# Moving the transfers of turned h, in the second gate/up product, from SyncE's queue to GpSimd's

## The chip, the core and the metric

One core of a Trainium2 chip runs the whole layer as one program. The metric is device time in microseconds (us), from start to end of the program. The kernel before takes 1830.62 us, the median of three runs (1828.49 to 1831.59).

The engines have short names here: PE (TensorE, matrix products), DVE (VectorE), ACT (ScalarE), POOL (GpSimd) and SP (SyncE, which only issues transfers). Each engine takes its instructions in the order of its own queue. A transfer (DMA) is issued from the queue of an engine and then runs beside it.

## The reference

A layer on x of 256 rows by 2048 columns in float32: half a feed-forward net, a mixer (a state-space group beside stick-breaking attention), half a feed-forward net again, and a gated per-layer embedding. The change lies in the second feed-forward net:

```python
def swiglu(h, w_gate, w_up, w_down):
    return (jax.nn.silu(h @ w_gate) * (h @ w_up)) @ w_down

x = x + 0.5 * swiglu(rms_norm(x, ffn2_norm[i]), ffn2_w_gate[i], ffn2_w_up[i], ffn2_w_down[i])
```

w_gate and w_up are 2048 x 5632, w_down is 5632 x 2048.

## The kernel before

**Halves.** A float32 product is made of three products of a rounded type: every operand is split in a high half (a cast on ACT, line 181) and a low half (what the cast lost, a subtraction on DVE, line 184). For weights the tiles are called whi/wlo or shi/slo, in seven pairs that are used in turn; raw is the weight tile as it came from memory (128 x 2048, 1 MB, five buffers). A raw buffer is free again when the last split that reads it has ended.

**Blocks.** Gate and up columns are worked in eleven blocks f = 0 to 10 of 512 columns each. In the second feed-forward net (`bg` is None there) the blocks from 1 on use the class `Wide`. Its `seven` takes a fast scheme with seven products in place of eight: weights of gate and up are added to each other on DVE (line 697, tile sum), one addition is made by an accumulating transfer from one raw buffer into another (line 704, from POOL's queue), and seven products run on PE (lines 666, 670 and 672). Between some products ACT hands a bank over with its sign turned (line 679). What is left of the 2048 rows is multiplied in the plain way by `column` (lines 325, 328 and 334): in even blocks two quarters of the rows, in odd blocks, where `seven` takes a third tile too ("joined"), one quarter.

**Loads.** Weights come through SP's queue: line 634 for the tiles of `seven`, line 315 for the columns, line 526 for the same in the down product.

**Order of a block.** `seven`, gate columns, up columns. When the gate columns are done, ACT applies silu (line 795, tile sg); when the up columns are done, DVE forms h = silu(gate) * up (lines 799 and 805).

**Steps.** Small pieces of work are put beside the products: `step()` is called after every product of `seven` and after every half of a column, and each generator in the list `beside` advances by one then. Steps set the place in program order only. The compiler orders each engine's queue itself, by its estimate of when things become ready, and may move a ready instruction ahead of one that waits.

**Turning h.** The down product needs h with its columns along the partitions. Two steps into the block after f, `turned` runs: DVE transposes h in squares of 32 (`turn_blocks`, line 217) into the tile mid. After each odd f, and after the last one, `turn_quarters` places the turned rows with 16 transfers of 32 partitions (line 230) into the tile hT of the pair of blocks. These transfers are issued in four groups of four, after 8 steps more. An even block has 7 + 8 = 15 steps, so the groups stand in its last four. mid has one buffer; hT is read by the down product only, as the tile hhi and others. `turn_quarters` is called from `Normed.block` too, for x (tile h, other step counts).

**After the gate/up product.** `fetch_x` (line 150) brings x back through POOL's queue, in eight transfers, into two of the five raw buffers; the down product runs with its own accumulating transfers (line 580) from POOL.

Of the kernel before, what the change touches and what calls it, by code (L numbers as in the profile page):

```python
# [33 lines left out]
def layer_kernel(ctx: ExitStack, tc: tile.TileContext, a: dict, shapes: dict, out: bass.AP):  # L34
    nc = tc.nc
# [31 lines left out]
    def get(pool, tag, width=1024, bufs=1):  # L67
        return pool.tile([P, width], F32, tag=tag, name=uid(tag), bufs=bufs)

    def com(tag):  # L70
        return get(comp, tag, *{"sg": (1024, 1), "h": (1024, 2), "sq": (NB, 1), "mid": (2048, 1)}[tag])
# [23 lines left out]
    def start(g):  # L95
        beside.append(g)
        return g
# [117 lines left out]
    def turn_blocks(mid, src, t, k0, nk):  # L215

        nc.vector.transpose(
            mid[:, :, t, k0 : k0 + nk, :].rearrange("p q f b -> p f q b"),
            src.rearrange("p (f q b) -> p f q b", f=nk, q=4),
        )  # L220

    def turn_quarters(out, mid, steps):


        def g():
            for _ in range(steps):
                yield
            for i in range(4):
                for q in range(4):
                    nc.sync.dma_start(  # L230
                        out[32 * q : 32 * q + 32].rearrange("p (t i w) -> p t i w", t=TT, i=4)[:, :, i],
                        mid[32 * i : 32 * i + 32, q].rearrange("p t f b -> p t (f b)"),
                    )
                yield

        return start(g())

    def by_tile(out, nk):

        return out.rearrange("p (x f b) -> p f x b", f=nk, b=32)  # L240
# [142 lines left out]
    class Normed:  # L383
# [12 lines left out]
        def block(self, n):  # L396
            if self.laid:
                ps = self.laid(n)
            elif n < self.early:

                if n % 2 == 0 or self.mid is None:
                    self.mid = com("mid")
                mid = self.mid[:, n % 2 * 1024 : n % 2 * 1024 + 1024].rearrange(
                    "p (q t f b) -> p q t f b", q=4, t=TT, b=32
                )
                out = com("h")
                for t in range(TT):
                    turn_blocks(mid, xt[t][n], t, 0, 4)
                soon = n >= ND - 2
                turn_quarters(out, mid, 4 if soon else 6)  # L410
                put_off(9 if soon else 11, self.parted, n, by_tile(out, 4))
                put_off(1, self.squares, n)
                return
            else:
                ps = aux()
                for t in range(TT):
                    for j in range(4):
                        pin(nc.tensor.transpose(
                            ps[:, j * T + t * P : j * T + (t + 1) * P], xt[t][n][:, j * P : (j + 1) * P], ident
                        ))  # L420
            self.parted(n, ps.rearrange("p (j s) -> p j s", j=4))
            if not self.laid:
                put_off(1, self.squares, n)
# [317 lines left out]
    def ffn(i, xn, nxt, bg=None):  # L741
# [11 lines left out]
        mids = {}  # L753
# [5 lines left out]
        def turned(hp, f, hh):  # L759
            pair, n_pair = f // 2, min(2, NF - f // 2 * 2) * 4  # L760
            if f % 2 == 0:
                mids[pair] = com("mid")[:, : 128 * TT * n_pair].rearrange(
                    "p (q t f b) -> p q t f b", q=4, t=TT, b=32
                )
            for t in range(TT):
                turn_blocks(mids[pair], hh[:, t * NB : (t + 1) * NB], t, f % 2 * 4, 4)
            if f % 2 or f == NF - 1:
                hf = get(hp, f"hT{pair}", T * n_pair)
                turn_quarters(hf, mids[pair], 8)
                hT.append(by_tile(hf, n_pair))  # L770

        for f in range(NF):
# [9 lines left out]
            if not bg and f:  # L782
# [10 lines left out]
                def gate(s=s, sg=sg):  # L793
# [6 lines left out]
                    out=hh.rearrange("p (t n) -> p t n", t=TT), in0=s.double.rearrange("p (t n) -> p t n", t=TT),  # L800
                    in1=five.unsqueeze(1).to_broadcast([P, TT, NB]), op=ALU.add,
                )
                for t in range(TT):
                    cols = slice(t * NB, (t + 1) * NB)
                    nc.vector.scalar_tensor_tensor(
                        out=hh[:, cols], in0=hh[:, cols], scalar=xn.rs(t), in1=sg[:, cols], op0=ALU.mult, op1=ALU.mult
                    )
                if f == NF - 2:
                    side.close()
                    hp = pools.enter_context(phase(f"h{i}b"))  # L810
                put_off(2, turned, hp, f, hh)
                continue
            if bg and (f >= early or f in alone):
# [28 lines left out]
                def ended(s, g=gate_cols, u=up_cols, hh=hh, f=f, hp=hp):  # L842
                    nc.vector.tensor_tensor(out=hh, in0=s.banks[3.8], in1=hh, op=ALU.add)
                    for t in range(TT):
                        nc.vector.scalar_tensor_tensor(
                            out=u[t], in0=u[t], scalar=xn.rs(t), in1=g[t], op0=ALU.mult, op1=ALU.mult
                        )
                    put_off(2, turned, hp, f, hh)
# [37 lines left out]
            for t in range(TT):  # L886
                nc.vector.scalar_tensor_tensor(
                    out=hh[:, t * NB : (t + 1) * NB], in0=pu[t], scalar=xn.rs(t),
                    in1=sg[:, t * NB : (t + 1) * NB], op0=ALU.mult, op1=ALU.mult,
                )  # L890
            put_off(2, turned, hp, f, hh)

        fetch_x(a["x"][0] if bg else scr_x)
# [805 lines left out]
    for n, side in ((0, 0), (1, 0), (0, 1), (1, 1), (2, 0), (2, 1), (3, 0), (3, 1)):  # L1699
        y, r = ((yss, rss), (ysb, rsb))[side]  # L1700
        ps = next(both) if n < 2 and not side else gemm_block(lambda k: y[k], sides[side], n * NB, SW // P)
        for t in range(TT):
            nc.vector.scalar_tensor_tensor(
                out=xt[t][n], in0=ps[t], scalar=r[0][:, t : t + 1], in1=xt[t][n], op0=ALU.mult, op1=ALU.add
# [127 lines left out]
    for c, (ahead, total) in enumerate(((early, part), (part, ms))):  # L1832
# [3 lines left out]
            out=com("sq")[:, :W], in0=gate[:, cols[c]], scalar=1.0, in1=gate[:, cols[c]], op0=ALU.mult, op1=ALU.mult,  # L1836
# [129 lines left out]
```

## Time and profile before

| | before |
|---|---|
| median of three runs | 1830.62 us |
| the profiled execution's own time | 1830.58 us |
| its span, first to last instruction | 1828.8 us |
| granted TensorE clock | 0.999 |
| PE busy | 1809.7 us (99%) |
| DVE busy | 1561.9 us (85%) |
| ACT busy | 1090.9 us (60%) |
| POOL busy | 110.9 us (6%) |

A row of a group or of a timeline reads: start, duration, engine, line, operation, tile written <- tiles read, shape, count, and in brackets the idle time of the engine before it with what ended that. Times are us from the start of the span. "SPq" is an issue on SP's queue. A row of waits reads: who waited <- for whom: total us, how often, the longest. A matmul row lasts 0.39 us but the next one starts 0.23 us after it: they are pipelined, so the distance of starts is what a matmul costs.

### The profile page before, as it was taken

What the parts mean: (1) busy time and instruction counts of PE and PEld (TensorE: products, weight loads), DVE (VectorE), ACT (ScalarE), POOL (GpSimd) and SP (SyncE); (2) the same over time, 40 slices, a digit from 0 to 9 for tenths busy, and PEclk for the clock granted to TensorE, in tenths of its full rate; (3) what the DMA queues carried; (4) which work ended last, traced back from release to release, by engine and by line L of the source; (5) the groups of instructions that cost most, each with busy time, mean ns of one, the idle gap of its engine ahead of it and who ended that gap; (6) DMA issues with size and microseconds to landing.
All of it is one profiled execution on the core that took longest, in us unless ns stands there. A gap on an engine that the chain in (4) does not pass through costs nothing.

```text
span 1828.8 us, 24199 instructions
## 1 busy us (share of the span) xinstructions
PE 1809.7 (99%) x8894; PEld 1492.1 (82%) x8894; DVE 1561.9 (85%) x1809; ACT 1090.9 (60%) x1282; POOL 110.9 (6%) x166
## 2 busy tenths in 40 slices
PE   9999999999999999999999999999999999999998
PEld 7888888888888888888898888777877788888887
DVE  8978889999998896696567889989898998889875
ACT  7445456555665665455794675666566756566664
POOL 0020100000000001010020000000000010000000
PEclk9999999999999999999999999999999999999999
DMA  8799866787775667574646778677777686666663
GB/s 323 268 293 302 262 213 230 239 273 219 254 281 200 203 235 257 178 260 150 225 142 225 250 240 294 220 262 231 247 234 242 224 281 232 230 201 225 207 236 127
DMA packets 108230, 430.49 MB, mean 235 GB/s; under 512 B 24432, under 2 KB 48400, under 8 KB 65712
## 3 DMA queue, kind: packets, MB, share of 16 engines
q1 hardware_dynamic: 96256, 390.06, 60.3%
q0 software_dynamic: 11136, 37.49, 9.5%
q8 instruction: 69, 1.13, 0.3%
q10 hardware_dynamic: 720, 1.41, 0.2%
q14 instruction: 49, 0.40, 0.1%
HBM read 372.41 MB, written 10.88 MB: 210 GB/s over the span
## 4 chain that ended last, share of the span: by engine, by line
PE 87%; DVE 5%; issue 3%; DMA 2%; ACT 2%; POOL 0%; ACTq 0%; DVEq 0%; POOLq 0%
PE acc L325 15%; PE acc L334 15%; PE acc L328 15%; PE aux L325 6%; PE aux L328 6%; PE aux L334 6%; PE acc L512 2%; PE acc L513 2%; PE acc L515 2%; DVE wlo L184 2%; PE acc L666 2%; PE aux L515 2%; PE acc L670 2%; PE aux L512 2%; PE aux L513 2%
## 5 line engine op out<-in xcount | busy, mean ns | idle before, releaser
L184 DVE TENSOR_TENSOR wlo<-raw,whi 128x1024 fp32r<-128x1024 f32 x483 | 584.0, 1222 | 132.1 <-ACT whi L181 131.7
L181 ACT CAST whi<-raw 128x1024 fp32r<-128x1024 f32 x483 | 502.0, 1050 | 304.0 <-PE acc L328 188.0
L325 PE MATMUL acc<-whi,nhi 128*128 128x512 f32 x880 | 346.5, 394 | 1.1 <-ACT whi L277 0.9
L328 PE MATMUL acc<-whi,nlo 128*128 128x512 f32 x880 | 343.6, 390 | 0.0
L184 DVE TENSOR_TENSOR slo<-raw,shi 128x1024 fp32r<-128x1024 f32 x183 | 222.4, 1215 | 32.1 <-ACT shi L181 31.0
L334 PE MATMUL acc<-wlo,nhi 128*128 128x512 f32 x880 | 243.8, 389 | 0.1
L181 ACT CAST shi<-raw 128x1024 fp32r<-128x1024 f32 x183 | 192.0, 1049 | 64.5 <-DMA raw<-in_ffn_w_down 17.7
L325 PEld LDWEIGHTS acc<-whi,nhi 128*128 128x128 f32 x880 | 165.7, 188 | 37.9 <-ACT whi L277 1.9
L334 PEld LDWEIGHTS acc<-wlo,nhi 128*128 128x128 f32 x880 | 165.3, 188 | 35.0 <-DVE wlo L184 0.5
L328 PEld LDWEIGHTS acc<-whi,nlo 128*128 128x128 f32 x880 | 165.8, 188 | 33.6
L181 ACT CAST whi<-sum 128x1024 fp32r<-128x1024 f32 x88 | 92.3, 1051 | 122.5 <-DVE sum L519 61.9
L184 DVE TENSOR_TENSOR wlo<-sum,whi 128x1024 fp32r<-128x1024 f32 x88 | 106.7, 1219 | 8.0 <-ACT whi L181 7.3
L181 ACT CAST shi<-sum 128x1024 fp32r<-128x1024 f32 x62 | 65.2, 1052 | 69.2 <-DVE sum L519 35.2
L325 PE MATMUL aux<-whi,nhi 128*128 128x512 f32 x216 | 84.0, 389 | 0.0
L328 PE MATMUL aux<-whi,nlo 128*128 128x512 f32 x216 | 84.0, 389 | 0.0
L184 DVE TENSOR_TENSOR slo<-sum,shi 128x1024 fp32r<-128x1024 f32 x62 | 75.6, 1219 | 1.3 <-ACT shi L181 1.0
L325 PE MATMUL aux<-whi,hhi 128*128 128x512 f32 x176 | 68.5, 389 | 0.0
L328 PE MATMUL aux<-whi,hlo 128*128 128x512 f32 x176 | 68.5, 389 | 0.0
L334 PE MATMUL aux<-wlo,nhi 128*128 128x512 f32 x216 | 65.2, 389 | 0.0
L519 DVE TENSOR_TENSOR sum<-sum,raw 128x1024 f32<-128x1024 f32 x50 | 61.0, 1220 | 0.8
L580 POOL DMA_DIRECT2D raw<-raw x23 | 19.9, 866 | 634.3 <-DVE sum L519 364.7
L697 DVE TENSOR_TENSOR sum<-sum,raw 128x1024 f32<-128x1024 f32 x50 | 58.4, 1217 | 0.0
(466 smaller groups left out, 3488.0 us busy)
## 6 DMA issues: line engine op xcount, KB each, us to landing
raw<-in_ffn_w_up SPq DMA_DIRECT2D x88, 1024.0 KB, 6.8
raw<-in_ffn_w_down SPq DMA_DIRECT2D x88, 1024.0 KB, 4.9
raw<-in_ffn_w_gate SPq DMA_DIRECT2D x86, 1024.0 KB, 6.9
raw<-in_w_in SPq DMA_DIRECT2D x32, 1024.0 KB, 5.4
raw<-raw POOLq DMA_DIRECT2D x50, 512.0 KB, 6.6
raw<-in_w_out SPq DMA_DIRECT2D x16, 1024.0 KB, 4.9
raw<-in_w_ple_gate SPq DMA_DIRECT2D x16, 1024.0 KB, 6.4
hT<-mid SPq DMA_DIRECT2D x160, 64.0 KB, 4.7
```

What stands on the lines that cost most here:

```text
L181: copy = nc.scalar.copy(hi, src)
L184: rest = nc.vector.tensor_tensor(out=lo, in0=src, in1=hi.bitcast(F32), op=ALU.subtract)
L325: nc.tensor.matmul(ps[t], lhsT=lh, rhs=hi[:, j, cols], start=start and j == 0, stop=False, skip_group_check=joined)
L328: nc.tensor.matmul(ps[t], lhsT=ll, rhs=hi[:, j, cols], start=False, stop=False, skip_group_check=joined)
L334: nc.tensor.matmul(ps[t], lhsT=lh, rhs=lo[:, j, cols], start=False, stop=stop and j == 1, skip_group_check=joined)
L512: nc.tensor.matmul(ps, lhsT=lh[j], rhs=hi[:, j], start=begin and j == 0, stop=False)
L513: nc.tensor.matmul(ps, lhsT=ll[j], rhs=hi[:, j], start=False, stop=False)
L515: nc.tensor.matmul(ps, lhsT=lh[j], rhs=lo[:, j], start=False, stop=z in final and j == 1)
L519: nc.vector.tensor_tensor(out=t, in0=x, in1=y, op=ALU.add)
L666: nc.tensor.matmul(ps, lhsT=lh[j], rhs=hi[:, j], start=fresh and i == 0 and j == 0, stop=False, skip_group_check=True,)
L670: nc.tensor.matmul(ps, lhsT=ll[j], rhs=hi[:, j], start=False, stop=False, skip_group_check=True)
L697: nc.vector.tensor_tensor(out=o, in0=u, in1=v, op=ALU.add)
```

## The change

`turn_quarters` gets a parameter for the queue, SP's by default. In the second feed-forward net the transfers go through GpSimd's queue, after 4 steps in place of 8. In the first net, and for x, nothing changes.

```diff
-    def turn_quarters(out, mid, steps):
+    def turn_quarters(out, mid, steps, queue=nc.sync):
...
             for i in range(4):
                 for q in range(4):
-                    nc.sync.dma_start(
+                    queue.dma_start(
                         out[32 * q : 32 * q + 32].rearrange("p (t i w) -> p t i w", t=TT, i=4)[:, :, i],
                         mid[32 * i : 32 * i + 32, q].rearrange("p t f b -> p t (f b)"),
                     )
...
                 hf = get(hp, f"hT{pair}", T * n_pair)
-                turn_quarters(hf, mids[pair], 8)
+                turn_quarters(hf, mids[pair], *((8,) if bg else (4, nc.gpsimd)))
                 hT.append(by_tile(hf, n_pair))
```

The 96 transfers of the second net (16 for each of the six pairs, the last pair of one block) are the ones that move. Tiles, shapes, bytes and arithmetic stay the same.

## The prediction

> **What bounds the kernel now.** I read the page's engine table first, then PE's own waits inside the stage that the change touches, then DVE and ACT there. The stage is the second gate/up product, from about 1030 to 1500 us of the span.
>
> ```profile
> PE 1809.7 (99%) x8894; PEld 1492.1 (82%) x8894; DVE 1561.9 (85%) x1809; ACT 1090.9 (60%) x1282; POOL 110.9 (6%) x166
> hT<-mid SPq DMA_DIRECT2D x160, 64.0 KB, 4.7
> ```
>
> PE is busy for 99% of 1828.8 us. Only PE's waits can be won, and the change lies in one stage. Its waits there, from the view of waits for PE between 1030 and 1500 us (total, times, longest):
>
> ```profile
> PE aux L672 <- DVE wlo L184: 7.0, 4, 1.8
> PE acc L666 <- ACT acc L679: 2.2, 3, 1.1
> PE acc L666 <- ACT aux L679: 1.2, 5, 0.3
> PE aux L672 <- DVE slo L184: 0.3, 1, 0.3
> ```
>
> Together 10.7 us in 13 waits. That is the ceiling for the idle time, and none of these waits names a weight transfer or a transfer of h. So a transfer that lands sooner wins nothing by itself; it must let DVE or ACT start something sooner. The largest row is four waits for DVE's low halves. Two neighbouring stretches show where DVE stands (columns: the stretch, its length, then busy time and instructions of PE, PEld, DVE, ACT, POOL):
>
> ```profile
> 1189.00:1231.00 42.00, 40.82 (x180) 33.13 (x179) 35.32 (x34) 26.18 (x30) 1.72 (x2) 1.00 0.81 271
> 1231.00:1273.00 42.00, 40.26 (x176) 32.61 (x175) 41.88 (x39) 26.95 (x29) 2.67 (x3) 1.00 0.66 212
> ```
>
> In the stretch of an odd block (f=5 here) DVE has no idle time, 41.88 of 42; in the even block before it (f=4) it idles 42 - 35.32 = 6.7 us. The two timelines of DVE and PE tell how that ends:
>
> ```profile
> 1222.06 1.21 DVE L184 TENSOR_TENSOR wlo<-raw,whi 128x1024 fp32r<-128x1024 f32 x1
> 1229.44 1.23 DVE L184 TENSOR_TENSOR slo<-raw,shi 128x1024 fp32r<-128x1024 f32 x1 [6.17 <-ACT shi L181]
> ...
> 1231.72 2.35 DVE L697 TENSOR_TENSOR sum<-raw,raw 128x1024 f32<-128x1024 f32 x2
> ...
> 1260.64 1.22 DVE L184 TENSOR_TENSOR wlo<-raw,whi 128x1024 fp32r<-128x1024 f32 x1
> ```
>
> ```profile
> 1259.55 0.39 PE L666 MATMUL aux<-whi,nhi 128*128 128x512 f32 x1
> 1259.78 0.39 PE L670 MATMUL aux<-whi,nlo 128*128 128x512 f32 x1
> 1261.91 0.73 PE L672 MATMUL aux<-wlo,nhi 128*128 128x512 f32 x2 [1.74 <-DVE wlo L184]
> ```
>
> DVE idles 6.17 us, starts at 1229.44 with a backlog, and PE then stands for the wlo that starts at 1260.64. Matmuls start 0.23 us apart when nothing waits (1259.55, 1259.78); here it is 2.13, so this wait costs **1.9 us**, and there is one in each of four odd blocks (f = 3, 5, 7, 9). DVE's idle time itself comes from ACT:
>
> ```profile
> 1219.16 1.06 ACT L181 CAST whi<-raw 128x1024 fp32r<-128x1024 f32 x1 [0.66 <-PE acc L328]
> 1226.42 0.69 ACT L795 ACTIVATE sg<-acc,sm 128x512 f32<-128x512 f32 x1 [6.20 <-PE acc L334]
> ...
> 1228.37 1.04 ACT L181 CAST shi<-raw 128x1024 fp32r<-128x1024 f32 x1
> ```
>
> ACT waits 6.20 us for PE's gate columns with the activation L795 at the head of its queue; the first casts of the next block stand behind it. At the other kind of border, odd to even, the order is different:
>
> ```profile
> 1184.29 1.06 ACT L181 CAST shi<-raw 128x1024 fp32r<-128x1024 f32 x1
> 1189.27 0.69 ACT L795 ACTIVATE sg<-acc,sm 128x512 f32<-128x512 f32 x1 [3.93 <-PE acc L334]
> ```
>
> There two casts of the next block (the one at 1184.29 is the second) come ahead of L795. And at the border f=0 to f=1, casts of the next block's raw and summed weights precede the activation, and block 1 loses nearly nothing at the place where the four others lose 1.9:
>
> ```profile
> 1063.92 1.05 ACT L181 CAST shi<-sum 128x1024 fp32r<-128x1024 f32 x1
> ...
> 1068.10 1.27 ACT L860 ACTIVATE sg<-aux,sm 128x512 f32<-128x512 f32 x2
> ```
>
> ```profile
> 1092.91 0.39 PE L670 MATMUL aux<-shi,nlo 128*128 128x512 f32 x1
> 1093.42 0.73 PE L672 MATMUL aux<-slo,nhi 128*128 128x512 f32 x2
> ```
>
> 0.51 between starts, so 0.28 us lost. What sets the four borders apart is what SP does just before them:
>
> ```profile
> 1187.27 4.90 SPq L315 DMA_DIRECT2D raw<-in_ffn_w_gate  x2
> 1202.89 3.79 SPq L230 DMA_DIRECT2D hT<-mid  x6
> 1207.40 0.33 SPq L315 DMA_DIRECT2D raw<-in_ffn_w_up  x1
> 1207.78 1.24 SPq L230 DMA_DIRECT2D hT<-mid  x2
> 1209.67 0.33 SPq L315 DMA_DIRECT2D raw<-in_ffn_w_up  x1
> 1210.05 7.88 SPq L230 DMA_DIRECT2D hT<-mid  x8
> 1218.03 0.53 SPq L634 DMA_DIRECT2D raw<-in_ffn_w_gate  x1
> ```
>
> Sixteen transfers of h go through SP in even blocks, and the next block's first weights (L634) are issued right as the last of them is out.
>
> **The change part by part.**
>
> *Taken from SP.* 96 issues (16 for each of the six pairs of blocks, by the code). Of the 16 of a pair, the eight at 1210.05 hold up L634. How long was its buffer free already? The five raw buffers come free as DVE's splits end. Issues at 1207.40 and 1209.67 follow such ends directly. Counting the splits in twos from there, the next buffer is free with this one:
>
> ```profile
> 1210.70 1.21 DVE L184 TENSOR_TENSOR wlo<-raw,whi 128x1024 fp32r<-128x1024 f32 x1
> ```
>
> at 1211.91. L634 was issued at 1218.03, so the first weights of an odd block can go **6.1 us** sooner, four times. Later loads of the block gain less and less, since their buffers come free later. The head of the queue wins nothing either: SP stood from 1192.17 (1187.27 + 4.90) to 1202.89 for DVE's transposes, and the up weights at 1207.40 waited for a buffer, not for SP.
>
> *Four steps sooner.* Worth 0: in the queue the transfers already stand ahead of their transposes. They cannot start before 1202.86 on any queue. Nor does anybody wait for their end: h is read in the down product; only the last pair is near its reader.
>
> *Added to POOL.* 16 issues per pair. Nearest rows, POOL's other 64 KB transfers and its accumulates in this stage:
>
> ```profile
> 100.25 3.87 POOL L1160 DMA_DIRECT2D coef<-scr_coef  x8 [2.33 <-DMA scr_coef<-cft]
> 1191.29 1.75 POOL L704 DMA_DIRECT2D raw<-raw  x2 [34.06 <-DVE sum L697]
> 1239.41 2.67 POOL L704 DMA_DIRECT2D raw<-raw  x3 [46.37 <-DVE sum L697]
> ```
>
> Bounds: 3.87/8 = 0.48 us and 1.75/2 = 0.88 us each; I take 0.48, the same size, so 7.7 us per pair (at most 14). The new wait on POOL is for the transposes (end 1202.86); behind it stands the next block's accumulate at 1239.41, and 1202.86 + 14 = 1217 leaves 22 us. The accumulates of the same block are issued 11 us ahead of them. At the end of the stage fetch_x and the down product's first accumulates share POOL; x is needed at the end of a column, and PE has no wait at all between 1470 and 1600 us (the view of its waits is empty there): it is fed from halves prepared ahead. Cost 0; without that cover the first accumulate would come up to 16 x 0.48 = 7.7 us late, once.
>
> *What 6.1 us sooner brings.* At the border of f=4 and f=5, ACT idles 6.20 us and DVE 6.17. With the first weights in place, two casts can stand ahead of L795, as at the odd-to-even border. Two low halves and the two sums at 1231.72 can then fill DVE's hole: 4 x 1.18 (2.35/2) = 4.7 us, more than the 1.9 that PE stands. Then that wait falls to what f=1 has. The order in the queues is the compiler's own, by its estimate of when things are ready, so this is not certain; that it put casts ahead where weights came early, and behind where they came late, is my reason to expect it.
>
> Sum, against the profiled execution (1830.58 us, its span 1828.8 and 1.8 around; the median shown is 1830.62, as good as equal): 4 x (1.9 - 0.28) = 6.5 gained, 0 for the rest: **1824.1 us**. Should DVE's lead carry on, the three waits of PE for L679 (2.2) and more of the 10.7 go too: with some 0.2 of refill per wait, at most 13, which gives 1817.6.
>
> The Trainium skill, "DMA: Bandwidth & Descriptors", section "Issuing engines are not separate DMA queues", says that transfers from any engine run on the same 16 DMA engines and that another issuer saves the sequencer's time alone, usually small. By that the sum would be 0 and the time 1830.6, the first rival; the row at 1210.05 speaks against "small" here: 7.88 us in which weights stand still.
>
> **The rivals.**
>
> *A. Nothing reaches PE (same).* The weights come 6.1 us sooner, but L795 stays ahead of the casts, or DVE, once ahead, only waits at L799 for PE's up columns. The loads of L634 take, from issue to landing (view of that line):
>
> ```profile
> DMA to landing us min/median/max: 4.7/7.4/11.9
> ```
>
> For it: no PE wait names a transfer, and even the late weights had landed (1218.03 + 7.4 = 1225.4) before ACT touched them at 1228.37. Against it: the odd-to-even and f=0 borders. Time 1830.6, and with up to 0.2% of shuffled queues 1827.0 to 1834.2.
>
> *B. The accumulates land later (slower).* The place: even blocks, where ACT waits for the accumulate from raw to raw. The chain of work that ended last holds it:
>
> ```profile
> 1191.29 0.86 POOL raw L704
> ...
> 1192.18 11.63 DMA raw<-raw
> ```
>
> It lands at 1203.81, one us after the transposes end. If those come sooner by more than one us and the accumulates do not, the 16 x 64 KB = 1 MB of h runs beside them. A 1 MB load takes 4.7 us at best (L634's row), so up to 4.7 us more, straight on PE in f = 4 and 8, where PE stood for L679 already: 1830.6 + 9.4 = 1840.0. Against it: the same DMA engines carry the same bytes as before, and the accumulate is ahead of h in POOL's queue.
>
> *C. POOL's descriptor writing and DVE hold each other up (slower).* 16 x 0.48 = 7.7 us of DVE per pair; its idle 6.7 in the even block takes most, 1.0 remains, and five pairs make 5: 1835.6; with 0.88 per issue 14 - 6.7 = 7.3, 37 in all. Against it:
>
> ```profile
> 1192.29 1.23 DVE L184 TENSOR_TENSOR wlo<-sum,whi 128x1024 fp32r<-128x1024 f32 x1 [0.52 <-ACT whi L181]
> ```
>
> This split ran while POOL issued the accumulate of 1192.18 (0.86 long) and took 1.23, against 1.22 elsewhere. The Trainium skill, "GPSIMD Engine Reference", section "Key points", has GpSimd and VectorE contend for their shared SBUF interfaces when a VectorE instruction has two SBUF inputs, as this one does; the trace shows no more than 0.01 us of it.
>
> **How the numbers follow.** Forecast 0.46 (1824.1, own range 1817.6 to 1827.0); A 0.38; B 0.10 (1840.0); C 0.06 (1835.6). A measurement of this kernel tells about 0.2% (3.7 us) from no change, so faster is below 1827.0: 0.46, same 0.38, slower 0.16. For 8 in 10 I leave out most of B and C and the last us of the forecast's low end: **1818.5 to 1834.5**.
>
> **What would show it.** Right: SP issues L634 near 1212 in f=4's place, no L230 there; two casts ahead of L795 at the even-to-odd borders; DVE's hole of 6.17 gone; PE's row "aux L672 <- DVE wlo L184" well under 7.0. A: L634 sooner, but the hole and the 7.0 as before. B: PE's waits for L679 above 2.2 and raw-to-raw landings above 11.63. C: L184 splits longer than 1.22 beside L230 on POOL. The prediction is wrong if the next block's weights were never held by SP, that is, if L634 stays near 1218.

## The result, and the profile after

| | before | after |
|---|---|---|
| median of five runs | 1830.62 us (1828.04 to 1831.59) | 1821.22 us (1820.74 to 1821.82) |
| ratio, 95% interval | | 0.9952 (0.9937 to 0.9967) |
| span of the profiled execution | 1828.8 us | 1819.0 us |
| PE's waits between 1020 and 1500 us | 10.7 us in 13 | 4.2 us in 9 |

The change makes the kernel 9.4 us faster; 1824.1 was forecast. Busy times from the page of the changed kernel:

```profile
PE 1805.6 (99%) x8894; PEld 1491.3 (82%) x8894; DVE 1564.4 (86%) x1809; ACT 1096.7 (60%) x1282; POOL 161.6 (9%) x262
```

PE, DVE and ACT have as many instructions as before, POOL 96 more. What changed for the three is order and waiting. PE's waits between 1020 and 1500 us:

```profile
PE acc L666 <- ACT aux L679: 2.5, 7, 0.9
PE acc L666 <- ACT acc L679: 1.7, 2, 0.9
```

The row of 7.0 us for DVE's low halves is gone. What is left is handing over by ACT (L679): 4.2 us, against 2.2 + 1.2 = 3.4 before. At the end of block 5, where PE had stood 1.9 us for wlo, its timeline now reads:

```profile
1256.31 0.39 PE L670 MATMUL aux<-whi,nlo 128*128 128x512 f32 x1
1256.54 0.62 PE L672 MATMUL aux<-wlo,nhi 128*128 128x512 f32 x2
...
1260.39 0.39 PE L328 MATMUL acc<-shi,nlo 128*128 128x512 f32 x1
1261.05 0.50 PE L666 MATMUL acc<-whi,hhi 128*128 128x512 f32 x1 [0.27 <-ACT aux L679]
```

The first two starts are 0.23 apart, so nothing is left of the wait for wlo. The last two are 0.66 apart: there PE loses 0.43 us at a handing over by ACT, a little further on. Now the places that were shown of before. The windows of the even block f = 4 and of the odd block f = 5:

```profile
1185.00:1227.00 42.00, 42.00 (x186) 34.47 (x185) 39.32 (x37) 27.73 (x32) 10.27 (x18) 1.00 0.87 281
1227.00:1268.00 41.00, 40.73 (x181) 33.38 (x180) 40.90 (x39) 26.84 (x28) 2.73 (x3) 1.00 0.71 225
```

In the even block DVE idles 42 - 39.32 = 2.7 us where it idled 6.7. PE is busy all the time there. SP, in its timeline, has weights alone:

```profile
1204.58 1.46 SPq L315 DMA_DIRECT2D raw<-in_ffn_w_up  x2
1207.98 0.33 SPq L634 DMA_DIRECT2D raw<-in_ffn_w_gate  x1
1212.52 0.33 SPq L634 DMA_DIRECT2D raw<-in_ffn_w_up  x1
1214.79 0.33 SPq L634 DMA_DIRECT2D raw<-in_ffn_w_gate  x1
1217.06 2.60 SPq L634 DMA_DIRECT2D raw<-in_ffn_w_up  x2
1226.51 0.33 SPq L634 DMA_DIRECT2D raw<-in_ffn_w_gate  x1
```

The first load of the next block goes out at 1207.98 where it went at 1218.03, the last at 1226.51 where it went at 1234.17 (the row is shown further down). ACT's timeline at the border has two casts of the next block ahead of the gate activation:

```profile
1218.66 1.06 ACT L181 CAST shi<-raw 128x1024 fp32r<-128x1024 f32 x1 [1.56 <-PE acc L328]
1221.38 1.06 ACT L181 CAST whi<-raw 128x1024 fp32r<-128x1024 f32 x1 [1.66 <-PE acc L328]
1223.19 0.69 ACT L795 ACTIVATE sg<-acc,sm 128x512 f32<-128x512 f32 x1 [0.76 <-PE acc L334]
```

The 6.20 us that ACT stood ahead of L795 are 0.76. DVE's waits, over the whole stage (1050 to 1500 us), first before, then after:

```profile
DVE slo L184 <- ACT shi L181: 17.2, 4, 6.2
DVE wlo L184 <- ACT whi L181: 14.3, 9, 6.3
DVE h L799 <- PE aux L334: 0.7, 1, 0.7
```

```profile
DVE sum L697 <- DMA raw<-in_ffn_w_up: 9.1, 5, 3.1
DVE wlo L184 <- ACT whi L181: 8.9, 11, 1.5
DVE h L799 <- PE aux L334: 0.8, 1, 0.8
DVE slo L184 <- ACT shi L181: 0.6, 3, 0.2
DVE nlo L184 <- ACT nhi L181: 0.3, 1, 0.3
```

32.2 us against 19.7. DVE's long waits behind an activation that waits for PE are gone; the largest row is now one for transfers that have yet to land. This sum is the number to follow through the experiments.

**Where the 9.4 us lie.** A matmul that starts d us after the one before it, with d over 0.3, loses d - 0.227. Summed over all starts in the traces that is 27.0 us before and 17.8 after, and of the 9.2 us between them 9.1 lie between 1050 and 1500 us (16.5 against 7.5). Of these 9.1 the four waits for wlo give 7.7 (4 x 1.92, to nothing), two waits for slo 0.4, and losses under 0.15 us 1.6 (29 of them to 14, over half of them right behind a larger one). Handing over at L679 takes 0.6 back (5.1 to 5.7 in sum): the waits of 1.12 us near 1208 and 1.27 near 1376 fell to nothing and 0.45, but others grew, as near 1124 from 0.33 to 1.07.

### The profile page after: what moved, and what is told of

Read it like the earlier page. It is cut to its first block, busy times and chain, and to the rows that moved or that the text cites. A ratio compares the mean times of both kernels' runs of the same rounds, so it can differ in the third digit from the quotient of the medians.

```text
span 1819.0 us, 24278 instructions
## 1 busy us (share of the span) xinstructions
PE 1805.6 (99%) x8894; PEld 1491.3 (82%) x8894; DVE 1564.4 (86%) x1809; ACT 1096.7 (60%) x1282; POOL 161.6 (9%) x262
## 4 chain that ended last, share of the span: by engine, by line
PE 89%; DVE 4%; DMA 2%; issue 2%; ACT 2%; SPq 0%; DVEq 0%; ACTq 0%
PE acc L325 15%; PE acc L334 15%; PE acc L328 15%; PE aux L325 7%; PE aux L328 7%; PE aux L334 7%; PE acc L666 3%; PE acc L670 2%; PE acc L672 2%; PE acc L512 2%; PE acc L513 2%; PE acc L515 2%; PE aux L515 1%; PE aux L513 1%; PE aux L512 1%
## 5 line engine op out<-in xcount | busy, mean ns | idle before, releaser
L181 ACT CAST whi<-raw 128x1024 fp32r<-128x1024 f32 x483 | 502.8, 1050 | 329.1 <-PE acc L328 194.4
L184 DVE TENSOR_TENSOR wlo<-raw,whi 128x1024 fp32r<-128x1024 f32 x483 | 584.0, 1222 | 127.5 <-ACT whi L181 126.9
L181 ACT CAST shi<-raw 128x1024 fp32r<-128x1024 f32 x183 | 192.2, 1050 | 80.7 <-DMA raw<-in_ffn_w_down 21.5
L184 DVE TENSOR_TENSOR slo<-raw,shi 128x1024 fp32r<-128x1024 f32 x183 | 222.5, 1216 | 15.2 <-ACT shi L181 14.7
L184 DVE TENSOR_TENSOR wlo<-sum,whi 128x1024 fp32r<-128x1024 f32 x88 | 106.8, 1219 | 7.4 <-ACT whi L181 6.8
L184 DVE TENSOR_TENSOR slo<-sum,shi 128x1024 fp32r<-128x1024 f32 x62 | 75.6, 1219 | 1.1 <-ACT shi L181 0.8
L697 DVE TENSOR_TENSOR sum<-sum,raw 128x1024 f32<-128x1024 f32 x50 | 59.5, 1220 | 0.7 <-DMA raw<-in_ffn_w_up 0.2
```

What stands on the lines that cost most here:

```text
L181: copy = nc.scalar.copy(hi, src)
L184: rest = nc.vector.tensor_tensor(out=lo, in0=src, in1=hi.bitcast(F32), op=ALU.subtract)
L697: nc.vector.tensor_tensor(out=o, in0=u, in1=v, op=ALU.add)
```

## The experiments

The theory: SP's issues for h held up the next block's weight loads; with these early, the compiler puts casts ahead of L795, DVE's idle time goes, and with it PE's waits. Against it stand four others: the steps do it; POOL as such does it; the early landing does it by itself; the order does it by itself. Where an edit adds lines, the line numbers of its rows are up by one to eight; the row's tiles say which line of the kernel it is.

| kernel | median us | ratio to before, 95% interval | DVE's waits 1050-1500, us |
|---|---|---|---|
| after | 1821.22 | 0.9952 (0.9937 to 0.9967) | 19.7 |
| POOL, 8 steps | 1821.12 | 0.9955 (0.9943 to 0.9968) | 20.7 |
| SP, 4 steps | 1830.04 | 1.0001 (0.9992 to 1.0009) | 32.5 |
| SP, 16 steps | 1819.07 | 0.9942 (0.9929 to 0.9954) | 18.8 |
| after, order as before | 1828.17 | 0.9995 (0.9986 to 1.0004) | 32.2 |
| before, gate activation late | 1829.28 | 0.9994 (0.9985 to 1.0003) | 31.4 |
| POOL for two pairs alone | 1824.42 | 0.9968 (0.9956 to 0.9981) | 24.2 |
| after, each transfer twice | 1830.69 | 1.0002 (0.9993 to 1.0011) | 34.4 |
| after, small second transfers | 1821.94 | 0.9956 (0.9942 to 0.9970) | 20.5 |

(The last column adds up the view of DVE's waits. One more kernel, POOL for everything, has its loss in another stage and stands below, as do two runs of a last comparison.)

### The queue or the steps

```diff
-                turn_quarters(hf, mids[pair], *((8,) if bg else (4, nc.gpsimd)))
+                turn_quarters(hf, mids[pair], *((8,) if bg else (8, nc.gpsimd)))
```

> The transfers of h stay in POOL's queue, but with 8 steps, as many as before. Theory: the four steps are worth nothing, the other queue alone does it. Then about 1821.5 us, within 2 us of the changed kernel, and PE's waits between 1020 and 1500 us stay near the 4.2 us in 9 of the changed kernel. Rival: the four steps carry the gain. Then it is back near 1830, with the 7.0 us of PE waits for DVE's wlo.

```diff
-                turn_quarters(hf, mids[pair], *((8,) if bg else (4, nc.gpsimd)))
+                turn_quarters(hf, mids[pair], *((8,) if bg else (4, nc.sync)))
```

> The other half of the change alone: four steps instead of eight, but the transfers stay in SP's queue. Theory: the steps are worth nothing and SP still holds up the weight loads, now with 16 transfers together ahead of the up loads instead of 8 and 8. Then about 1830, between 1828 and 1834, and ACT still idles some 6 us ahead of L795 in odd blocks' borders. Rival: the steps carry the gain. Then about 1821.

POOL with 8 steps: 1821.12 us, as the changed kernel. SP with 4 steps: 1830.04, as before. So the steps are worth nothing and the queue everything. In the second kernel PE's waits are those of before:

```profile
PE aux L672 <- DVE wlo L184: 7.1, 4, 1.8
```

and SP's timeline shows the 16 transfers in one piece, now ahead of the up weights:

```profile
1203.27 10.19 SPq L230 DMA_DIRECT2D hT<-mid  x16
1213.62 0.97 SPq L315 DMA_DIRECT2D raw<-in_ffn_w_up  x2
1214.69 0.38 SPq L634 DMA_DIRECT2D raw<-in_ffn_w_gate  x1
```

L634 is 3.3 us sooner here than before, but the first up weights ahead of it are 6 us later, and the two together gain nothing. One load's place in time is no measure of the whole.

### On SP, but behind the loads

```diff
-                turn_quarters(hf, mids[pair], *((8,) if bg else (4, nc.gpsimd)))
+                turn_quarters(hf, mids[pair], *((8,) if bg else (16, nc.sync)))
```

> The transfers stay in SP's queue, but 16 steps late, so that 10 of the 16 stand behind the next block's six loads of L634 and hold up none of them. Theory 'held weights' (what counts is that nothing stands ahead of the next block's loads when a buffer comes free, whatever the queue): 1821 to 1824, L634 issued before 1214, ACT's idle before L795 near the 8.4 us in 7 of the changed kernel. Rival 'another queue is needed' (SP's issues cost wherever they stand, or POOL's queue itself brings something): 1828 to 1831.

1819.07 us, below the range that was expected: the whole gain, with POOL not used. SP's timeline:

```profile
1200.03 3.79 SPq L230 DMA_DIRECT2D hT<-mid  x6
1204.54 1.47 SPq L315 DMA_DIRECT2D raw<-in_ffn_w_up  x2
1207.94 0.33 SPq L634 DMA_DIRECT2D raw<-in_ffn_w_gate  x1
...
1223.84 0.33 SPq L634 DMA_DIRECT2D raw<-in_ffn_w_gate  x1
1224.22 10.06 SPq L230 DMA_DIRECT2D hT<-mid  x10
```

Six transfers use the time in which SP would wait for a raw buffer, and ten stand behind all six loads. L634 goes at 1207.94, as in the changed kernel. What counts is that none of h's transfers stands ahead of a load whose buffer is free. The Trainium skill, "DMA: Bandwidth & Descriptors", section "Issuing engines are not separate DMA queues", says that all issuers share the same DMA engines and that a second one saves issue time alone, usually a small one. The first half agrees with this run: another queue brings nothing that a later place on SP does not bring. "Small" does not hold for before: eight issues, which with the waits between them took 7.88 us, stood ahead of 1 MB loads.

### Early landing without the new order

The changed kernel, where the casts of b11 in the odd blocks from 3 to 9 wait for the previous block's gate activation, and the sums for the second split:

```diff
-            p = self.prepare(b11)
+            with tc.issue_after(self.held) if self.held else nullcontext():
+                p = self.prepare(b11)
...
-            add(b11, b12)
+            with tc.issue_after(self.rests[1]) if self.held else nullcontext():
+                add(b11, b12)
```

> The changed kernel, transfers in POOL's queue, weights early; but in the odd blocks f = 3, 5, 7, 9 the casts of the first operand are held behind the previous block's silu gate (L795) and the sums behind the second split, so that ACT and DVE work in the order of the kernel before. Theory 'order': the early weights pay only because the compiler then puts two casts ahead of L795; without that about 1828 to 1831, ACT idle some 6 us ahead of L795, and PE's row for DVE wlo back at about 7 us. Rival 'arrival': the earlier landing pays by itself, about 1821.

1828.17 us, not to be told from before. Of block 5's loads the first goes out at 1212.36 (1218.03 before) and the second at 1216.90 (1218.66), the next three as before; all five land 1.3 to 2.0 us sooner than before (in the changed kernel 3.7 to 4.7, of which 2.8 are its head start). But ACT stands ahead of the gate activation (here L799) again, and PE waits for wlo as it did:

```profile
1226.48 0.69 ACT L799 ACTIVATE sg<-acc,sm 128x512 f32<-128x512 f32 x1 [5.75 <-PE acc L334]
```

```profile
PE aux L673 <- DVE wlo L184: 6.6, 4, 1.7
```

So loads that go out and land sooner are worth nothing by themselves: "arrival" falls.

### The new order at L795 without early landing

The kernel before, where in blocks 2, 4, 6 and 8 the gate activation and L805 are written in the next block, behind two casts of its b11:

```diff
             p = self.prepare(b11)
             self.multiply(b2, "11", p, True)
+            if late:
+                with tc.issue_after(self.copies[1]):
+                    late()
             add(b11, b12)
...
-                put_off(0, gate)
+                if joined or f == NF - 1:
+                    put_off(0, gate)
...
+                    def late(gate=gate, formed=formed, f=f, hp=hp, hh=hh):
+                        gate()
+                        formed()
+                        put_off(2, turned, hp, f, hh)
```

> The kernel before, transfers in SP's queue in 8 steps, weights as late as ever; but at the borders from an even to an odd block (f = 2, 4, 6, 8) the silu gate (L795) and the product of L805 are written down in the next block, behind two casts of its first operand. Theory 'order': 1822 to 1826 even with the late weights, since these landed (about 1225) before ACT could end L795 as it stood (1228), though two casts may wait some us for them. Rival 'arrival': the casts now wait for the late weights and L795 behind them too, 1830 or more.

1829.28 us: the theory as put there missed. The order came out as meant (casts at 1224.33 and 1225.29, the activation at 1226.82), and DVE's hole of 6.17 us closed to 1.11. But DVE's timeline shows others in its place (L805 in it is the kernel's L799):

```profile
1225.42 1.23 DVE L184 TENSOR_TENSOR slo<-raw,shi 128x1024 fp32r<-128x1024 f32 x1 [1.11 <-PE acc L334]
...
1227.70 2.35 DVE L698 TENSOR_TENSOR sum<-raw,raw 128x1024 f32<-128x1024 f32 x2
1231.57 1.23 DVE L184 TENSOR_TENSOR wlo<-sum,whi 128x1024 fp32r<-128x1024 f32 x1 [1.52 <-ACT whi L181]
1234.29 1.23 DVE L184 TENSOR_TENSOR wlo<-sum,whi 128x1024 fp32r<-128x1024 f32 x1 [1.49 <-ACT whi L181]
...
1239.06 1.23 DVE L805 TENSOR_TENSOR h<-aux,sq 128x1024 f32<-128x1024 f32 x1 [1.27 <-PE aux L334]
```

1.11 + 1.52 + 1.49 + 1.27 = 5.4 us, so only 0.8 of the 6.2 is gained, and PE waits for wlo four times, 7.1 us, as before. The changed kernel has sums in such places (DVE's L697 at 1221.85, 1224.13 and 1227.54). Here their weights were late: the third and fourth load went out at 1220.25 and 1222.06 and the fifth behind them, against 1214.79 to 1219.34 in the changed kernel, and the fourth and fifth took 10.4 and 11.1 us to land, until 1232.4 and 1235.4. But their order was not that of the changed kernel either. In blocks 3, 5, 7 and 9 the changed kernel has the last three sums ahead of L799, in block 5 from 1229.92 on; this run, like before, has them behind it, at 1242.65. So the run does not tell whether the sums lacked the landing or the order.

The border from f = 2 to f = 3 tells more. There the changed kernel has no lead yet: the up weights go at 1123.22, before at 1123.32. The first load of block 3, first before, then in the changed kernel:

```profile
1132.38 0.53 SPq L634 DMA_DIRECT2D raw<-in_ffn_w_gate  x1
```

```profile
1127.76 0.33 SPq L634 DMA_DIRECT2D raw<-in_ffn_w_gate  x1
```

It goes out 4.6 us sooner, but takes 10.2 us to land in place of 5.3, and so lands 0.3 us later. The second lands 0.3 later too, the next three 0.7 to 1.2 sooner. Yet DVE's idle time at this border falls from 5.4 us to 1.2, and PE's wait for wlo goes from 1.92 us to nothing. What did change is the order: two casts ahead of L795, and these last sums, first before, then in the changed kernel, where they stand ahead of L799:

```profile
1157.58 3.49 DVE L697 TENSOR_TENSOR sum<-sum,raw 128x1024 f32<-128x1024 f32 x3
```

```profile
1148.54 1.23 DVE L697 TENSOR_TENSOR sum<-sum,raw 128x1024 f32<-128x1024 f32 x1 [0.19 <-DMA raw<-in_ffn_w_up]
```

So here the gain came with the order, at nearly the same landing. What stands is that PE's waits go only with the compiler's other order, of the sums as well as of the casts, and that the compiler made it in every kernel where h does not hold up the next block's loads, unless it was held. That it did so because it reckoned with earlier loads is likely but not shown, and whether this whole order, written down with h's transfers left as they were, would bring the gain was not run.

### Two pairs alone

```diff
-                turn_quarters(hf, mids[pair], *((8,) if bg else (4, nc.gpsimd)))
+                turn_quarters(hf, mids[pair], *((4, nc.gpsimd) if not bg and pair in (1, 3) else (8,)))
```

> The change for two of the pairs alone: the transfers of pairs 1 and 3 (blocks 2 and 3, 6 and 7) go through POOL's queue four steps sooner, all others stay on SP with 8 steps. Theory 'a held border each': of the four PE waits of 1.8 us for DVE's wlo, the two behind the changed pairs (odd blocks f = 5 and 9, near 1262 and 1430 us) go, those near 1177 and 1346 stay, and the time is halfway, 1824 to 1827. Rival: the gain comes from the whole queue being free (a lead that carries over from block to block), then one pair left on SP spoils most of it, 1828 or more, or the waits stay in other places than named.

1824.42 us, in the range named. PE's waits over the stage:

```profile
PE aux L672 <- DVE wlo L184: 3.5, 2, 1.8
```

Two of four are left. They lie in the stretches 1145 to 1185 us (1.7) and 1310 to 1355 us (1.8), as named; in the odd blocks behind the moved pairs there are none. Each pair of transfers moved pays for the block behind it, and what is left on SP costs its full wait there. The order goes with it: the last three sums stand ahead of L799 in blocks 5 and 9, and behind it in 3 and 7. Half of the pairs bring 6.4 us (1830.81, the runs of before beside it, less 1824.42), more than half of the whole.

### Prices on POOL and on the DMA engines

Each transfer of the second net issued twice on POOL, the copy going to a scratch tensor:

```diff
-                    queue.dma_start(
-                        out[32 * q : 32 * q + 32].rearrange("p (t i w) -> p t i w", t=TT, i=4)[:, :, i],
+                    for to in (out, twice)[: 1 + bool(queue is nc.gpsimd)]:
+                        queue.dma_start(
+                            to[32 * q : 32 * q + 32].rearrange("p (t i w) -> p t i w", t=TT, i=4)[:, :, i],
```

> The changed kernel with every transfer of h issued a second time on POOL, the copy going to a scratch tensor in DRAM that nobody reads: 32 issues a pair instead of 16, another 1 MB a pair on the DMA engines. It prices what the prediction's rivals B and C feared. Theory: POOL and the DMA engines have room, within 4 us of the changed kernel (1819 to 1825). If C's mechanism is there, DVE's L184 beside POOL's issues is longer than 1.23 and the time is 5 us or more longer; if B's, the landing of the accumulates from raw to raw rises above 11.6 and PE's waits for L679 above the 4.2 us.

1830.69 us, 9.5 more than the changed kernel: the theory's range missed. Which mechanism? Not C: the splits of DVE take what they took, from the view of L184 (min/median/max in ns; 1178/1216/1226 in the changed kernel):

```profile
L184 DVE TENSOR_TENSOR wlo<-raw,whi x100: 1177/1215/1227, 1050.2 to 1498.2; 128x1024 fp32r<-128x1024 f32 x100
```

The Trainium skill, "GPSIMD Engine Reference", section "Key points", has GpSimd and VectorE contend when a VectorE instruction has two SBUF inputs, as these have; with 32 issues a pair on POOL nothing of it shows. Nor B as the prediction put it: the accumulates land 4.7/8.4/12.3 us after issue (min/median/max), against 4.8/8.4/11.5 in the changed kernel. What grew is the waiting for weights, by who waited for the loads of `seven` (L699 is the kernel's L697, which waited 9.1 us in 5 waits in the changed kernel):

```profile
  DVE sum L699: 17.3, 12
```

To tell bytes from issues, the second copy was cut to 16 of the 256 numbers of a row:

```diff
+                    if queue is nc.gpsimd:
+                        again = twice[32 * q : 32 * q + 32].rearrange("p (t i w) -> p t i w", t=TT, i=4)[:, :, i]
+                        queue.dma_start(again[:, :, :16], of[:, :, :16])
```

> As the run with every transfer of h issued twice on POOL, but the second copy moves 16 of the 256 numbers of each row only: 32 issues a pair as there, with the bytes of one and a sixteenth. Theory 'bytes': what cost the doubled kernel 9.5 us over the changed one was the second MB a pair on the DMA engines, which lets the weight loads land later; then this one is near the changed kernel, 1821 to 1824. Rival 'queue': it was POOL's 24 us of issues a pair, which hold up the accumulates behind them; then it is near the doubled one, 1828 to 1831, and POOL's first accumulate of an odd block is issued as late as there.

1821.94 us, which speaks for the bytes. One reserve: the compiler put the small copies into the next block (16 at 1243.43 us), so the issues of a pair are doubled but not in one piece, and what is copied runs beside other work. That a piece of 24 us on POOL is harmless isn't shown; in the run with full copies POOL's first accumulate of the odd block was, however, not held by it: POOL idled 6.89 us ahead of it, for DVE's sum.

### POOL for all transfers of turned quarters

```diff
-    def turn_quarters(out, mid, steps, queue=nc.sync):
+    def turn_quarters(out, mid, steps, queue=nc.gpsimd):
```

> The changed kernel with the transfers that place turned quarters sent through POOL's queue everywhere, the first gate/up net and the other turned tensors included, with the steps as they were there (8). Theory: outside the second net PE never waited for what SP's queue held up, so about 1821, within 2 us of the changed kernel. Rival: the same border wait is in the first net too, then some us less, 1812 to 1818; or POOL's other work there is held up, then more.

1842.76 us, 0.7% slower than before (1.0067, 1.0055 to 1.0080): the theory missed. PE's losses, counted by starts as above, are 17.8 us in the changed kernel and 41.0 here. Between 1000 and 1150 us they are 2.1 and 16.4, so 14 of these 23 us lie there, where x is turned and read at once; the rest is spread and wasn't followed. ACT's waits there (1000 to 1080 us), then PE's timeline:

```profile
ACT nhi L192 <- DMA h<-mid: 20.2, 2, 10.6
```

```profile
1039.45 0.67 PE L325 MATMUL aux<-whi,hhi 128*128 128x512 f32 x1 [2.62 <-ACT whi L181]
1063.54 0.79 PE L325 MATMUL aux<-whi,nhi 128*128 128x512 f32 x1 [5.88 <-ACT whi L181]
```

The same move that is free where the reader is far (hT, read in the down product) lands in PE's path where it is near (h, read by L192 at once). POOL issued the 16 for one half of x from 1044.93 to 1056.85 us, with waits for earlier transfers between them.

### Late on SP against early on POOL

The changed kernel once more, and beside it SP with 18 steps:

```diff
-                turn_quarters(hf, mids[pair], *((8,) if bg else (4, nc.gpsimd)))
+                turn_quarters(hf, mids[pair], *((8,) if bg else (18, nc.sync)))
```

> The changed kernel unaltered, on the same chip and against the same runs of before as the next one, so that the two can be compared: 1820 to 1822.

> SP's queue again, as in the run with 16 steps, but 18 steps late: 10 of a pair's 16 transfers stand behind the next block's six weight loads all the same, only the last pair differs. Theory: late on SP is a little better than early on POOL, since the transfers of h no longer run beside the accumulates of the same block and the next block's loads; then 1818 to 1820, some 2 us under the changed kernel beside it. Rival: the 2 us between the run with 16 steps and the changed kernel were chance; then 1820 to 1822 for both.

1820.43 us (0.9948, 0.9935 to 0.9962) and 1819.48 us (0.9936, 0.9924 to 0.9949). Late on SP is at least as good as POOL; the 1 to 2 us between them are within what the runs scatter, so that it is better isn't settled.

## The prediction, step by step

*What bounds the kernel.* Right. The four waits for wlo were the largest row and came from DVE's idle time before them; where that idle time stays (order as before, gate activation late, 4 steps on SP) they stay, and where it goes for one block they go for that block.

*Taken from SP.* Right, and so was the count of the buffer. The split that was counted out, the sixth behind the transposes, ends at 1207.95 in the changed kernel, and L634 goes at 1207.98:

```profile
1206.73 1.22 DVE L184 TENSOR_TENSOR wlo<-raw,whi 128x1024 fp32r<-128x1024 f32 x1
```

Of the 10.1 us by which the load goes sooner (1218.03 to 1207.98), 6.1 are what SP held it, and 4.0 are that this split itself ends sooner (1211.91 to 1207.95): 2.8 are a head start that DVE already had at the transposes, from the border before, and the rest is a sum that no longer stands ahead. At the other three borders the load was held 4.5, 7.2 and 6.7 us, counted in the same way. The loads behind it gain 6.1, 4.4, 4.0 and 4.0 us, less and less as forecast, but the last one gains 7.7 (1234.17 to 1226.51), since the split that frees its buffer ends sooner too. The row of before:

```profile
1234.17 0.33 SPq L634 DMA_DIRECT2D raw<-in_ffn_w_gate  x1
```

Two things the prediction did not see. The hold is not all issuing: the row of 7.88 us at 1210.05 has eight issues of 0.6 us each and 2.9 us in which SP waited for up weights to land. Over 1050 to 1500 us the view of SP's waits has:

```profile
SPq L230 <- DMA raw<-in_ffn_w_up: 13.7, 8, 3.3
```

And sooner out is not as much sooner in: the load at 1207.98 took 10.3 us to land, the one at 1218.03 4.9, so 4.7 of the 10.1 us are left. With 16 steps on SP, where most of h goes later, the same load (1207.94) took 6.7.

*Four steps sooner: 0.* Right (1821.12 and 1830.04).

*Added to POOL: 0.* Right. An issue took 8.57/16 = 0.54 us, not 0.48, in this row, which also shows that the next accumulate came 20 us later:

```profile
1200.39 8.57 POOL L230 DMA_DIRECT2D hT<-mid  x16 [11.08 <-DVE mid L217]
1229.34 2.73 POOL L704 DMA_DIRECT2D raw<-raw  x3 [20.37 <-DVE sum L697]
```

*What 6.1 us sooner brings.* The chain (loads early, two casts ahead of L795, low halves and sums in DVE's hole) is what the trace shows. The reason given was too narrow: two casts ahead of L795 do not do it. With these alone, DVE's hole only split into four. The sums, the last three of a block too, had to come ahead of L799, and in the changed kernel they do. That the weights land sooner is not what decides at the first border, where they hardly do. The new order itself was a guess from two other borders, called uncertain in the prediction, and it came out.

*The sum.* This is the step that was off: 4 x (1.9 - 0.28) = 6.5 and "0 for the rest". The four waits gave 7.7, since nothing is left of them; the 0.28 taken from block 1 is a wait for slo, which stayed where it was (1093.42 before, 1093.30 after). The rest was not 0 but 1.4: 1.6 from the short losses and 0.4 from two waits for slo, less 0.6 at L679. The far end of the range, 1817.6, had PE's waits for L679 going too "should DVE's lead carry on". The lead did carry on (the up weights go 2.8, 6.1 and 7.7 us sooner at the second, third and fourth border), but these waits moved and grew, from 3.4 to 4.2 us in the view. DVE's idle time fell by 12.5 us over the stage, some 3 a border, and the sum counted only the 1.6 of each that it gave to one wait of PE.

*The rivals.* A, nothing reaches PE: what it said of L795 staying ahead is what the run with the order of before shows, at 1828.17. So A hung on the compiler's order, and with 0.46 for the forecast and 0.38 for A the prediction hardly chose between the two. B: its marks are not there (accumulates land 4.8/8.4/11.5 us after issue, 4.6/8.5/11.6 before), but the waits for L679 are 0.8 us more in sum. C: no trace of it, with twice the issues either. More traffic does cost, with another megabyte a pair, and what grew then are the waits for weights and not the landing of the accumulates.

## What to carry to other kernels

Small transfers in the queue of the large loads cost what stands behind them: look for a load whose buffer is free while the queue issues something nobody waits for, and move that something behind the loads or to another queue; either will do. A load that goes out sooner may land hardly sooner, and paid here only together with another order of the engines' work, so look at which work the compiler then puts ahead of a wait, on each engine. Before moving a transfer to a queue where it lands later (between 1100 and 1480 us a median of 5.9 us on POOL in the changed kernel, of 4.8 on SP before), ask how far its reader is: the same move was free for hT and cost 14 us where x went along.

## What the runs showed of the chip

POOL issues a 64 KB transfer of this shape in 0.54 us (8.57/16), SP in 0.64 (10.19/16, with 4 steps), so POOL isn't the slower issuer. Neither queue ever has more than eight transfers under way in these traces: an engine that is eight ahead issues the next one when the one eight places before it has landed. In the changed kernel POOL stood so for 2.63 us ahead of the sixteenth:

```profile
1130.06 0.55 POOL L230 DMA_DIRECT2D hT<-mid  x1 [2.63 <-DMA hT<-mid]
```

In the kernel before SP stood so for 2.54 us ahead of its sixteenth, which went at 1217.35 as the up weights of 1209.67 had landed (7.7 us). Where those ahead land fast it doesn't show: with 4 steps on SP (a median of 2.1 us to landing) all 16 went out in one piece. The transfers of a queue use eight semaphores in turn, so this may well come from the program; that the chip has such a limit isn't shown.

With x on POOL, PE's waits of 2.62 and 5.88 us were followed by a lower granted clock, 0.93 in the window from 1050 to 1100 us where it was 1.00 in the changed kernel (the column behind POOL's):

```profile
1050.00:1100.00 50.00, 44.12 (x188) 36.08 (x187) 37.18 (x37) 29.16 (x35) 6.46 (x10) 0.93 0.72 227
```

Whether the waits alone lower it wasn't tried.
